# Two gate chunks moved to the mixer's entry, and way-up weights two tiles ahead with their low parts on GpSimd

## The chip, the cores and the metric

The kernel runs on one core of a Trainium2 chip. The metric is the device time of one execution in microseconds (us), the median of several runs. The core's engines work from separate instruction queues, each in order: TensorE (PE, its weight loads PEld), VectorE (DVE), ScalarE (ACT), GpSimd (POOL) and SyncE (SP), which here issues the DMAs.

## The reference

One step of a diffusion backbone with a single layer, on 1024 latent and 128 context tokens of width 1024 (1152 columns together, since the kernel keeps everything transposed). In short:

```python
x = x + 0.5 * m[2] * swiglu(modulate(x, norm_g[0], m[0], m[1]), *ffn1)
mix, ctx = token_mixer(modulate(x, norm_g[1], m[3], m[4]), ...)
x = x + m[5] * mix
x = x + 0.5 * m[8] * swiglu(modulate(x, norm_g[2], m[6], m[7]), *ffn2)
```

and in the token mixer

```python
qc, kvc, kr, hq, hf_f, hf_b, hi, hgate, ga, gr = split(h @ w_in)
...
merged = sigmoid(ga) * (o_attn @ w_up_attn) + sigmoid(gr) * (o_rec @ w_up_rec)
out = merged @ w_out
```

`o_attn` is softmax attention over compressed keys, `o_rec` a gated linear scan in both directions (HGRN2) with 8 heads, made from the projections hq (called q in the kernel), hf (f), hi (v) and hgate. ga and gr are the merge gates.

## The kernel before, in words

All matrices are float32. A product is made of three matmuls: each operand is split into a high part (a cast to fp32r on ACT) and a low part (the difference, on DVE or GpSimd), and high x high, high x low and low x high are added up in PSUM (`mm3`). A weight is so loaded by a DMA into a buffer `raw` (two of them), cast by ACT into `wh`, and subtracted into `wl` (three buffers each). `load_w` and `hl` do this; with `home="low"` or `"pieces"` the differences are on DVE in two halves.

The program is written as Python generators that yield after each piece; the order in which they are advanced is the order of the program. A planner then gives each engine its fixed order: of the instructions that its timing model holds ready, the one that stands first in the program. Buffers are reused by tags with a count; an instruction that writes into a buffer waits until the last one's readers are done.

**The mixer's entry** (`hgrn`). The 1152 columns are worked in three chunks of 384, in the order 2, 0, 1. The norm of the last chunk, 1, is still in work when the mixer begins: `self.tail` makes, one block of 128 rows at a time (8 steps), `xn` (L488, DVE), the high part `xh` (L489, ACT) and the low part `xl` (L490, DVE). Meanwhile TensorE makes the projections f, q and v of the first head pair. A projection chunk (`dense_g`, called by `proj_g`) is 24 matmuls of 384 columns in two halves of 12; it writes a PSUM bank of the tag `mm` (two banks) or, for some of the first chunks, `lv` (three). `rest` lists the order after f's and v's chunk 2: q and v and f and q by half chunks, up to v, f, q of chunk 1. The first eight half chunks of `rest` also advance `self.tail` by one step each, and from half chunk 11 on the scan's preparation `scan_pre` (its steps depend on f and q alone). Banks are read by ACT's sigmoid (L739) and, for q, also by DVE's product (L767); for v by a copy into a tile `t` (L778).

**The scan.** After `rest` the 8 heads are scanned in three chunks each. A scan step has small matmuls (L1068 with operands `KE`, `QP` from DVE, L1105), and between them `slots(k)` advances a chain of pending projections, `work`, by k half chunks: 7 or 8 in a step. `work_of(h)` lists what is in work for head h: the next head's f, at odd heads also the next pair's q and v, the output gate of a finished pair, and merge gates from `sgs` (16 generators `proj_sg`, each one weight and three chunks: sigmoid on ACT, stored to DRAM). What is left of the chain after the last scan step is run at the end, with the splitting of way-up weights for later (`split_up`), and then the last pair's output gate.

**The merge.** For each of 8 tiles m of 128 output rows, `up(m)` takes four quarters of 288 columns. The attention part is 12 matmuls of 288 columns, the recurrent part another 12 or, for two quarters, is read from DRAM as `mu`. DVE multiplies with the gates g and adds (L1688, L1690), ACT casts into `mh` (L1691), GpSimd makes `ml` (L1692). The weights of tiles 0 to 2 are loaded during attention; from then on `load_up_all` (L1425 to L1433) loads one: a DMA into `raw` (L1428), whose cast (L1677, ACT) and difference (L1678, DVE) make the first half of the weight, and two DMAs from DRAM (L1431), which bring the second half already split. After tiles 3 and 5, `down_group` adds two tiles' product with `w_out` to x: 192 matmuls, whose results DVE adds to x (L569) from three banks. `w_out`'s weights take the same `raw`, `wh` and `wl` buffers.

Of the kernel before, what the change touches and what calls it, by code (L numbers as in the profile page):

```python
# [21 lines left out]
KT = D // P  # L22
# [71 lines left out]
class Trunk:  # L94
# [761 lines left out]
    def hgrn(self):  # L856
        nc, pin = self.nc, self.tc.keep_in_program_order
        self.mmb = 2
        for tag, n in (("lv", 3), ("mm", 2), ("sm", 3)):
            self.pp.tile([P, 512], F32, tag=tag, bufs=n, name=tag)  # L860
        f32 = lambda n, sh: self.fp.tile(sh, F32, name=n)
        A, B = slice(0, 64), slice(64, P)
        self.kr = {m: f32(f"kr{m}", [P, CW]) for m in (8, 16, 32, 64)}
        self.XY = [f32(n, [P, 48, 8]) for n in "XY"]
        self.A1 = [f32(f"A1_{i}", [P, 3, G]) for i in range(2)]
        self.A2 = f32("A2", [P, 3, G])
        self.cnt, self.later, self.sigs = 0, [], []
        heads = [{} for _ in range(H)]
        pairs = [{} for _ in range(4)]
        sgs = [self.proj_sg(j) for j in range(2 * KT)]  # L870

        def feed(h):
            p = h // 2
            r = [self.proj_f(5 * p + h % 2, h, heads[h])]
            if h % 2 == 0:
                r += [self.proj_q(5 * p + 2, pairs[p]), self.proj_v(5 * p + 3, pairs[p])]
            return r

        def scan_of(h):
            p = h // 2  # L880
            if h % 2 == 0:
                pairs[p]["o"] = self.tt(F32, "oT")
            d = heads[h]
            d["pair"] = pairs[p]
            d["h"], d["QP"], d["As"] = h, self.tt(F32, "QP"), {}
            d["Gall"] = self.fp.tile([P, 9], F32, tag="Gall", bufs=2, name="Gall")
            return d

        def work_of(h):
            p = h // 2  # L890
            work = feed(h + 1) if h + 1 < H else []
            if h and h % 2 == 0:
                work = work + [sgs.pop(), self.beside(sgs.pop(), pairs[p - 1])]
                work += [self.proj_gate(5 * p - 1, p - 1, pairs[p - 1])]
            while len(work) < 4 - (h == 3) + (h == H - 1):
                work.append(sgs.pop())
            return chain(*work)

        pre = iter(())
        f, q, v = feed(0)  # L900

        def root_hook():
            next(v)
            next(self.tail)

        self.root_hook = root_hook
        for _ in range(2):
            next(f)
        next(v)

        def rest():
            for g in (q, v, f, q, v, f, q):
                for _ in range(2):
                    yield next(g)

        for i, _ in enumerate(rest()):
            if i < 8:
                next(self.tail)
            if i == 11:
                assert next(self.tail, 1)  # L920
                for t in self.XY:
                    pin(nc.vector.memset(t[:, :, 3:4], 1.0))
                d = scan_of(0)
                pre = self.scan_pre(d, ORDER[0])
            if i == 13:
                for t in self.A1 + [self.A2] + list(self.kr.values()):
                    pin(nc.vector.memset(t, 0.0))
            next(pre, None)
        for _ in pre:
            pass  # L930
        self.group()
        work = chain.from_iterable(map(work_of, range(H)))
        old = cur = out = last = None
        for p in range(H * NCH + 1):
            h, n = divmod(p, NCH)
            old, cur, pre = cur, None, iter(())
            if h < H:
                cur = self.scan_lev(d, ORDER[n])
            if p + 1 < H * NCH:
                h1, n1 = divmod(p + 1, NCH)  # L940
                while min(heads[h1].get("nf", 0), pairs[h1 // 2].get("nq", 0)) <= n1:
                    next(work)
                if n1 == 0:
                    last, d = d, scan_of(h1)
                pre = self.scan_pre(d, ORDER[n1])

            def slots(k):
                for _ in range(k):
                    next(work, None)
                    next(pre, None)  # L950

            self.group(old, cur)
            slots(3)
            self.group(old, cur, old, out)
            slots(2 + p % 2)
            self.group(cur, out, old)
            out = None
            if p and n == 0:
                out = self.scan_out(last if h < H else d)
                next(out)  # L960
            slots(2)
            for _ in pre:
                pass
        self.group(out, out)
        todo = list(range(KT // 2))
        for i, _ in enumerate(work):
            if i % 2 == 0 and todo:
                self.split_up(todo.pop(0))
        for p in todo:
            self.split_up(p)  # L970
        for n, _ in enumerate(self.proj_gate(19, 3, pairs[3])):
            if n == 0:
                self.group()
# [666 lines left out]
    def merge(self):  # L1640
        nc, a = self.nc, self.a
# [7 lines left out]
        def load_g(n=1):  # L1649
            for m, c in islice(parts, n):  # L1650
                g = self.half("g").rearrange("p (i n) -> p i n", i=2)
                pin(nc.sync.dma_start(g, self.sg[:, m, :, slice(*c)].rearrange("i p n -> p i n")))
                mu = None
                if REC[0] <= c[0] < REC[1]:
                    mu = self.fp.tile([P, QW], F32, tag="mu", bufs=4, name="mu")
                    pin(nc.sync.dma_start(mu, self.ahead[m][:, c[0] - REC[0] : c[1] - REC[0]]))
                gates.append((g, mu))

        def load_x(n):
            for k in range(len(self.x), min(len(self.x) + n, KT)):  # L1660
                t = self.tt(F32, f"x{k}")
                pin(nc.sync.dma_start(t[:, :T], self.xs[k]))
                self.x.append(t)

        def up(m):
            mh, ml = self.wide("mh", F32R), self.wide("ml", F32R)
            wh, wl = self.ups.pop(0)
            if m == 0:
                load_g(4)
            for n, c in enumerate(QORDER if m else first):  # L1670
                cs = slice(*c)
                g, mu = gates.pop(0)
                load_g()
                load_x(1)
                if 1 < m < KT - 1 and n == 0:
                    wh1, wl1, raw = self.load_up_all(m + 1)
                    nc.scalar.copy(wh1[:, :4], raw)  # L1677
                    nc.vector.tensor_sub(wl1[:, :4], raw, wh1[:, :4])  # L1678
                    self.ups.append((wh1, wl1))
                mt = []  # L1680
                for i in (1, 0):
                    if i and mu:
                        ps = mu
                    else:
                        ps = self.bank("up", "ups")
                        self.mm3(ps, [(wh[:, k], wl[:, k], *[t[:, cs] for t in hl[k]]) for k in range(4 * i, 4 * i + 4)])
                    t = self.fp.tile([P, QW], F32, tag="hf", bufs=3, name="mt") if i else ps
                    nc.vector.tensor_mul(t, ps, g[:, i])  # L1688
                    mt.append(t)
                nc.vector.tensor_add(mt[0], mt[1], mt[0])  # L1690
                nc.scalar.copy(mh[:, cs], mt[0])  # L1691
                nc.gpsimd.tensor_sub(ml[:, cs], mt[0], mh[:, cs])  # L1692
            return mh, ml
# [3 lines left out]
        for m in range(KT):  # L1697
            if m % 2 and m < KT - 1 and len(pend) > 1:
                homes = None, partial(self.tt, F32R)
                ws = [self.load_w(wo[f], 1, D, home=home, eng=nc.vector) for (f, _), home in zip(pend, homes)]  # L1700
            elif m == KT - 1:
                early = {i: self.load_w(wo[pend[i][0]], 1, D, home=homes[i], eng=nc.vector) for i in range(2)}
            pend.append((m, up(m)))
            if m % 2 and m < KT - 1 and len(pend) > 2:
                fs, hs = zip(*pend[:2])
                self.down_group(wo, fs, hs, 5, ws)
                pend = pend[2:]
# [742 lines left out]
```

## Time and profile before

| | us |
|---|---|
| median of three runs | 2833.44 |
| lowest and highest | 2833.11, 2836.21 |
| the profiled execution | 2831.82 |
| its span, first to last instruction | 2830.0 |

The profiled execution's mean granted TensorE clock is 0.995. TensorE is busy for 2763.6 us, DVE for 2037.8, ACT for 1302.9, GpSimd for 926.4. A row of the timeline has the start in us from the span's start, the duration in us, the engine, the line, the operation, the tile written and the tiles read, the shapes and the count; in brackets stand the engine's idle time before it and what ended it. A row of the waits reads: who waited for whom, us in total, times, the longest. A row of the groups reads: line, engine, operation, tiles, shape, count, then busy us, mean ns of one, then idle us before them with what ended most of it.

### The profile page before, as it was taken

Reading aid. Unit: us, or ns where it says so; the run is one execution under the profiler, and the core shown is the slowest. Engines: PE = TensorE matmul, PEld = TensorE weight load, DVE = VectorE, ACT = ScalarE, POOL = GpSimd, SP = SyncE. Lnnn points to the kernel's source line nnn. Section 1 sums busy time; section 2 is a strip of 40 time slices with the busy share of each in tenths; the row PEclk is TensorE's granted clock in tenths of the full one; section 3 lists DMA queues with packets and bytes.
Section 4 is the critical chain, followed back from the end, with each engine's and each line's share of the span. In section 5 each row is a group of like instructions: output and inputs, shape, how many; then the busy total and the mean of one; then the engine's idle time right before and its main releaser. Section 6 shows DMA issues by size and latency. Waiting matters only on the chain. (4 is left out here: it accounts for less than half of the span.)

```text
span 2830.0 us, 55726 instructions
## 1 busy us (share of the span) xinstructions
PE 2763.6 (98%) x21222; PEld 2633.5 (93%) x21222; DVE 2037.8 (72%) x4464; ACT 1302.9 (46%) x2696; POOL 926.4 (33%) x980
## 2 busy tenths in 40 slices
PE   8999999999999999999999999999999999999998
PEld 7999999999999998889998778689999999999997
DVE  7867777677678787877356777766766765568875
ACT  6533332321176676666436777741552322234332
POOL 0233232444222222222244444420414443423451
PEclk9999999999999999999999999999999999999999
DMA  6743443753121111112512001263454444358521
GB/s 261 228 130 118 130 125 118 260 180 117 57 82 57 45 63 38 66 41 84 192 60 98 19 15 30 84 232 104 154 171 130 145 156 134 116 164 253 164 85 67
DMA packets 219578, 337.64 MB, mean 119 GB/s; under 512 B 23664, under 2 KB 141360, under 8 KB 219312
## 3 DMA queue, kind: packets, MB, share of 16 engines
q1 hardware_dynamic: 219312, 334.10, 36.0%
q8 instruction: 167, 2.74, 0.4%
q14 instruction: 99, 0.81, 0.1%
HBM read 248.47 MB, written 85.54 MB: 118 GB/s over the span
## 5 line engine op out<-in xcount | busy, mean ns | idle before, releaser
L1902 PE MATMUL b<-xo,wo 128*128 128x288 f32 x3552 | 482.9, 295 | 0.0
L1902 PEld LDWEIGHTS b<-xo,wo 128*128 128x128 f32 x3552 | 474.8, 188 | 0.0
L1902 PE MATMUL b<-bh,wo 128*128 128x288 f32 x1776 | 366.0, 295 | 0.0
L539 PE MATMUL mm<-xh,wh 128*128 128x384 f32 x936 | 327.2, 350 | 5.5 <-DVE q L767 4.3
L541 PE MATMUL mm<-xh,wl 128*128 128x384 f32 x936 | 317.2, 339 | 0.0
L540 PE MATMUL mm<-xl,wh 128*128 128x384 f32 x936 | 316.6, 338 | 0.0
L1902 PEld LDWEIGHTS b<-bh,wo 128*128 128x128 f32 x1776 | 288.7, 188 | 0.0
L569 DVE SCALAR_TENSOR_TENSOR x<-dn,modt,x 128x256 f32<-128x256 f32 (+4 forms) x472 | 225.6, 499 | 83.8 <-PE dn L541 81.8
L1902 PE MATMUL b<-bl,wo 128*128 128x288 f32 x888 | 261.7, 295 | 0.0
L1876 ACT CAST wo<-raw 128x512 fp32r<-128x512 f32 x185 | 114.8, 621 | 221.1 <-issue 88.1
L539 PEld LDWEIGHTS mm<-xh,wh 128*128 128x128 f32 x936 | 176.4, 188 | 12.9 <-DVE q L767 5.5
L2103 PE MATMUL d<-xd,wd 128*128 128x288 f32 x1344 | 181.7, 297 | 5.0 <-DVE x L2090 3.0
L2103 PEld LDWEIGHTS d<-xd,wd 128*128 128x128 f32 x1344 | 180.0, 190 | 6.5 <-issue 4.4
L1877 DVE TENSOR_TENSOR wo<-raw,wo 128x512 fp32r<-128x512 f32 x185 | 127.4, 689 | 79.1 <-ACT wo L1876 76.5
L540 PEld LDWEIGHTS mm<-xl,wh 128*128 128x128 f32 x936 | 176.7, 189 | 0.9
L541 PEld LDWEIGHTS mm<-xh,wl 128*128 128x128 f32 x936 | 177.0, 189 | 0.0
L1599 POOL TENSOR_TENSOR ehl<-e,ehl 128x512 fp32r<-128x512 f32 x93 | 123.9, 1337 | 154.6 <-ACT ehl L1597 83.6
L393 DVE SCALAR_TENSOR_TENSOR junk<-wada,cb 128x512 bf16<-128x512 f32 x224 | 163.9, 732 | 5.5 <-DMA wada<-in_w_aT 4.6
L1902 PEld LDWEIGHTS b<-bl,wo 128*128 128x128 f32 x888 | 167.5, 189 | 0.0
L1872 POOL TENSOR_TENSOR ws<-raw 128x256 f32<-128x256 f32 x74 | 64.5, 892 | 283.1 <-DMA raw<-in_w 254.3
L539 PE MATMUL ps<-bh,wh 128*128 128x288 f32 (+1 forms) x448 | 135.7, 303 | 3.2 <-ACT bh L532 1.9
L1877 DVE TENSOR_TENSOR wo<-ws,wo 128x512 fp32r<-128x512 f32 x74 | 69.6, 940 | 92.4 <-ACT wo L1876 91.9
(477 smaller groups left out, 7163.9 us busy)
## 6 DMA issues: line engine op xcount, KB each, us to landing
raw<-in_w SPq DMA_DIRECT2D x148, 256.0 KB, 3.5
wada<-in_w_aT SPq DMA_DIRECT2D x112, 256.0 KB, 3.1
raw<-in_w SPq DMA_DIRECT2D x42, 512.0 KB, 3.8
raw<-in_w_in SPq DMA_DIRECT2D x41, 512.0 KB, 3.5
xr<-xd SPq DMA_DIRECT2D x56, 288.0 KB, 3.8
hr<-hs SPq DMA_DIRECT2D x26, 576.0 KB, 5.7
hb<-hd SPq DMA_DIRECT2D x44, 288.0 KB, 3.8
hs<-et SPq DMA_DIRECT2D x84, 144.0 KB, 2.3
```

What stands on the lines that cost most here:

```text
L393: nc.vector.scalar_tensor_tensor(junk, ws[n % 2], 1.0, cs[s], ALU.mult, ALU.mult, accum_out=o)
L539: pin(nc.tensor.matmul(ps, wh, xh, start=start and i == 0, stop=False))
L540: pin(nc.tensor.matmul(ps, wh, xl, start=False, stop=False))
L541: self.last_mm = nc.tensor.matmul(ps, wl, xh, start=False, stop=stop and i == n - 1)
L569: nc.vector.scalar_tensor_tensor(self.x[m][:, a:b], ps[:, a - lo : b - lo], self.modt[:, gm, m, s : s + 1], self.x[m][:, a:b], ALU.mult, A ...
L1599: eng.tensor_sub(el, e, eh)
L1872: nc.gpsimd.tensor_tensor(o[:, c], x[:, c], y[:, c], op)
L1876: nc.scalar.copy(wh, src[i])
L1877: nc.vector.tensor_sub(wl, src[i], wh)
L1902: nc.tensor.matmul(ps, w[:, k], x[:, k, :QW], start=first, stop=last, skip_group_check=home != i)
L2103: nc.tensor.matmul(ps, w[:, k], xv, start=start, stop=stop, skip_group_check=home != i)
```

## The change

In the mixer's entry one merge gate (`fill`) is taken from the list of 16, and four half chunks of it, that is its chunks 2 and 0, are put into `rest` ahead of v's, f's and q's chunk 1. Its third chunk stays, as the first gate in head 0's work. In the merge the weights of tiles 3 and 4 are loaded in tiles 1 and 2 instead of 2 and 3; those of tiles 5 to 7 stay where they were. All five differences go from DVE to GpSimd.

```diff
@@ work_of
                 work += [self.proj_gate(5 * p - 1, p - 1, pairs[p - 1])]
+            if not h:
+                work.append(fill)
             while len(work) < 4 - (h == 3) + (h == H - 1):
                 work.append(sgs.pop())
@@ hgrn
         next(v)
 
+        fill = sgs.pop()
+
         def rest():
-            for g in (q, v, f, q, v, f, q):
+            for g in (q, v, f, q, fill, fill, v, f, q):
                 for _ in range(2):
                     yield next(g)
@@ merge, up
-                if 1 < m < KT - 1 and n == 0:
-                    wh1, wl1, raw = self.load_up_all(m + 1)
+                if m in (1, 2, 4, 5, 6) and n == 0:
+                    wh1, wl1, raw = self.load_up_all(m + (2 if m < 3 else 1))
                     nc.scalar.copy(wh1[:, :4], raw)
-                    nc.vector.tensor_sub(wl1[:, :4], raw, wh1[:, :4])
+                    nc.gpsimd.tensor_sub(wl1[:, :4], raw, wh1[:, :4])
                     self.ups.append((wh1, wl1))
```

## The prediction

> **What bounds the kernel now.** I read the page first, then the busy time by stages, then the waits of TensorE inside the stages that the change touches, and last the engines' order in time around each wait.
>
> ```profile
> span 2830.0 us, 55726 instructions
> PE 2763.6 (98%) x21222; PEld 2633.5 (93%) x21222; DVE 2037.8 (72%) x4464; ACT 1302.9 (46%) x2696; POOL 926.4 (33%) x980
> ```
>
> TensorE is busy for 98% of the span, and the change neither adds nor removes a matmul. So only three things can pay: TensorE's idle time, stretches in which its granted clock is low, and new waits. The profiled execution took 2831.8 us, 1.8 us more than its span; the median of the runs is 2833.4. I make the sum against the profiled one and take the difference off the median. A measurement of this kernel can tell about 0.2% from no change, 5.7 us.
>
> The stages at the mixer's entry, from the view of busy time by window (window, its length, busy time and instructions of PE, PEld, DVE, ACT, POOL, granted clock, DMA):
>
> ```profile
> 832.26:840.68 8.42, 8.42 (x50) 8.42 (x49) 7.13 (x18) 4.31 (x10) 1.33 (x3) 1.00 0.01 2
> 840.68:849.46 8.78, 6.77 (x26) 4.74 (x25) 6.16 (x16) 4.52 (x8) 0.00 (x0) 0.83 0.00 0
> 849.46:859.64 10.18, 10.18 (x50) 10.14 (x49) 7.94 (x17) 7.07 (x14) 2.33 (x4) 0.81 0.00 1
> 859.64:879.64 20.00, 18.02 (x190) 16.58 (x189) 19.24 (x49) 13.94 (x32) 5.24 (x7) 1.00 0.08 28
> 880.64:884.06 3.42, 3.42 (x11) 3.42 (x12) 2.69 (x9) 3.33 (x8) 1.63 (x4) 0.50 0.34 122
> ```
>
> The first window holds f's and q's chunk 0: 48 matmuls in 8.42 us, 0.175 each. The second is v's chunk 1, the first work on the last chunk of the normed input: 24 matmuls that should take 4.2 us take 8.78, 4.6 lost. In the third, f's and q's chunk 1 take 10.18 instead of 8.42, 1.8 lost to a clock of 0.81. In the fourth TensorE idles 2.0 us while DVE is busy for 19.24 of 20, and the fifth runs at half clock: 1.7 lost. Who ended these waits, in the view of waits (the first two lines at the last chunk, the third in the scan's first steps):
>
> ```profile
> PE lv L539 <- ACT xh L489: 1.6, 3, 0.7
> PE lv L540 <- DVE xl L490: 0.4, 2, 0.2
> PE lv L1068 <- DVE QP L1105: 1.9, 2, 1.7
> ```
>
> TensorE runs out of normed input first, then of the scan's operands from DVE. The merge, in windows from the end of its third tile on, and its waits:
>
> ```profile
> 1890.50:1892.78 2.28, 0.16 (x2) 0.00 (x1) 1.23 (x4) 0.95 (x2) 0.93 (x2) 1.00 1.10 377
> 1892.78:1902.16 9.38, 9.38 (x71) 9.38 (x71) 6.73 (x12) 2.33 (x3) 1.10 (x2) 1.00 0.43 142
> 1902.16:1906.35 4.19, 3.30 (x24) 2.86 (x22) 3.50 (x9) 1.82 (x4) 2.57 (x3) 1.00 0.89 262
> 1906.35:1929.60 23.25, 23.25 (x175) 23.25 (x175) 15.83 (x36) 1.96 (x3) 0.00 (x0) 1.00 0.38 134
> 1948.90:1955.84 6.94, 5.04 (x39) 4.81 (x37) 3.99 (x10) 1.49 (x3) 2.42 (x3) 1.00 0.92 289
> 1955.84:1959.25 3.41, 3.41 (x15) 3.41 (x16) 1.62 (x5) 0.00 (x0) 0.00 (x0) 0.50 0.79 254
> ...
> PE ups L539 <- ACT wh L1677: 2.1, 1, 2.1
> PE dn L539 <- DVE x L569: 1.9, 1, 1.9
> PE ups L541 <- DMA wl<-wrec: 0.9, 1, 0.9
> PE ups L539 <- DVE mt L1690: 0.4, 1, 0.4
> ```
>
> A tile's way-up takes about 9.4 us, a matmul of the down group 23.25 / 175 = 0.133. Idle are 2.1 us ahead of tile 3, 0.9 in the window of tile 4's first matmuls, 0.4 later, 1.9 in the second down group, which a half-clock stretch follows (1.7 more).
>
> **Part 1: two gate chunks ahead of the last chunk.** Moved are 48 matmuls (8.4 us), their weight load of one DMA, one ACT cast and two DVE differences, two sigmoids on ACT and two stores on SP. The same work leaves the scan's filler later, so the matmuls cost nothing by themselves; the question is how much idle time they fill. They are long enough for all of it: v's chunk 1 would start at 840.7 + 8.4 = 849.1, when its input is complete. But the moved chunks write the two banks named mm, which f's and q's chunk 0 hold until ACT and DVE have read them:
>
> ```profile
> 841.96 0.47 ACT L739 ACTIVATE sg<-mm 128x384 f32<-128x384 f32 x1
> 848.51 0.55 DVE L767 TENSOR_TENSOR q<-mm,sg 128x384 f32<-128x384 f32 x1
> ```
>
> ACT and DVE run in a fixed order, and there these reads stand behind steps of the last chunk's norm, which the change leaves where it is. If that order stays, the first moved chunk starts at 841.96 + 0.47 = 842.4 instead of 840.7 (1.7 us of waiting) and ends at 846.6; the second waits for 848.51 + 0.55 = 849.1 (2.4 us). So 4.1 us of idle time stay.
>
> Whether the clock drops as well depends on how the wait falls. In the merge 1.9 us of idle time in the 6.9 us ahead were enough for a stretch of 3.41 us at 0.50. I count half of one such stretch, 0.85. Of 4.6 + 1.8 = 6.4 lost, 5.0 remain: a gain of 1.4, between 0.6 (a whole slow stretch) and 6.4 (the reads come earlier). [...]
>
> A cost on the other side: the third weight buffer now holds the moved gate, so the next f's weights, loaded ahead today, wait for v's last matmul. There are then 48 matmuls (8.4 us) of f and q to hide a cast, two differences and the queues; I put it at 0, with 1 us as the lower bound below. On SP the two stores wait for the sigmoids; behind them queue only loads of weights that are used after q's chunk 1.
>
> **The scan's first steps.** DVE is late there:
>
> ```profile
> 866.88 0.36 DVE L1075 COPY_PREDICATED A<-mask,lv 128x96 f32<-128x96 uint8 x2
> ```
>
> This reads products that TensorE makes right behind q's chunk 1, from 859.64 on, so DVE comes some 6 to 7 us late; it does the preparation of scan chunk 0 and the memsets first. With TensorE 8.4 us later at that point, DVE has done these by then. I count 2.5 of the 2.0 + 1.7 = 3.7 us as gained, between -1 and 3.7.
>
> **The rest of the scan.** Each scan step takes a fixed number of half chunks from the row of pending projections, so its amount of work stays; but all that follows comes four half chunks earlier, and meets another state of DVE. The waits between 900 and 1385:
>
> ```profile
> PE mm L539 <- DVE q L767: 4.3, 3, 2.3
> PE lv L1068 <- DVE QP L1105: 3.0, 4, 1.4
> PE ops L1164 <- ACT kT L1122: 1.6, 2, 0.8
> PE vt L785 <- ACT t L778: 1.3, 2, 0.7
> ```
>
> These 10.2 us are redrawn; I take 0 with 4 us either way. At the scan's end the leftover is four half chunks shorter:
>
> ```profile
> 1385.44:1398.16 12.72, 12.72 (x72) 12.56 (x72) 0.00 (x0) 1.47 (x3) 1.00 0.88 314
> ...
> 1392.56 1.29 DVE L346 TENSOR_TENSOR wl<-raw,wh 128x512 fp32r<-128x512 f32 x2 [7.62 <-ACT wh L342]
> ```
>
> Of the 72 matmuls 12 are the last gate's first half; it starts at 1385.44 + 60 x 0.175 = 1395.9, and its weights are ready at 1393.85. Needed 8.4 us earlier, they would be 6.3 us late if their load stayed. But that load hangs on weight buffers which earlier gates release, and these also come 8.4 us of TensorE's work earlier. I take 0, at worst -6.3.
>
> **Part 2: weights of tiles 3 and 4 two tiles ahead.** Tile 3's load today:
>
> ```profile
> 1882.44 0.33 SPq L1428 DMA_DIRECT2D raw<-in_w_up  x1
> ```
>
> It moves up by one tile of 9.4 us on SP, to about 1873: three DMAs among the g and x loads. Its buffer is free since tile 0. Its cast and difference then lie under tile 2, and the 2.1 us go. Tile 4's load, today ahead of tile 3's end, goes up by one tile too, and the 0.9 us go. Queued behind these DMAs on SP are loads of g for four quarters ahead; three issues of 0.3 to 0.4 us do not reach them. What is late next is the first down group's weights: they take the buffers that tile 2 and the loads ahead of them release. I leave 0.5 us for that.
>
> **Low parts on GpSimd.** The five differences, and what waits today:
>
> ```profile
> L1678 DVE TENSOR_TENSOR wl<-raw,wh x5: 691/692/866, 1892.8 to 1954.6; 128x512 fp32r<-128x512 f32 x5
>   ACT wh L1677: 7.0, 5
> ...
>   DMA raw<-in_w_up: 9.6, 3
> ...
> 1954.57 0.69 DVE L1678 TENSOR_TENSOR wl<-raw,wh 128x512 fp32r<-128x512 f32 x1 [2.56 <-ACT wh L1677]
> 1955.18 1.49 DVE L569 SCALAR_TENSOR_TENSOR x<-dn,modt,x 128x288 f32<-128x288 f32 x4
> ...
> L1599 POOL TENSOR_TENSOR ehl<-e,ehl x93: 1270/1291/2828, 1539.1 to 1856.8; 128x512 fp32r<-128x512 f32 x93
> L1692 POOL TENSOR_TENSOR ml<-mt,mh x32: 791/807/967, 1867.7 to 2000.8; 128x288 fp32r<-128x288 f32 x32
> ```
>
> DVE stood 7.0 us idle ahead of these five, each time for ACT's cast, and ACT stood 9.6 us ahead of three of the casts for their DMA. At 1954.57 four results of the down group queue behind one; with three banks full TensorE stops for 1.9 us and its clock halves for 1.7. On GpSimd the same difference takes 1.3 us (the same shape at L1599) against 0.69; behind it only ml differences of 0.8 us queue, which the next down group needs, one or two tiles later. So 1.9 + 1.7 + 0.4 go. Together the merge gains 2.1 + 0.9 + 0.4 + 1.9 + 1.7 - 0.5 = 6.5, between 4 and 7.
>
> [...]
>
> ```profile
> L1688 DVE TENSOR_TENSOR mt<-mu,g 128x288 f32<-128x288 f32 x16 | 8.8, 567 | 0.7 <-POOL ml L1692 0.7
> L1688 DVE TENSOR_TENSOR mt<-ups,g 128x288 f32<-128x288 f32 x16 | 7.3, 456 | 7.7 <-PE ups L541 7.7
> ```
>
> The product with both inputs in SBUF takes 567 ns beside GpSimd's ml, the one with a PSUM input 456. Five differences of 1.3 us could hold DVE for 6.5 us at most; DVE is busy for 6.73 of 9.38 us in tile 3's window, so 1.3 us in a tile fits.
>
> **Sum.** 1.4 + 2.5 + 0 + 6.5 = 10.4 us: 2831.8 becomes 2821.4, the median 2833.4 becomes 2823.
>
> **Rivals.** (a) The reads of the two banks come early, since they alone hold TensorE: entry and first steps pay in full, 6.4 + 3.7 + 6.5 = 16.6, 2817. For it: ACT is idle for 4.3 of 8.78 us there. Against it: the norm's steps keep their place. (b) The scan gives back what the entry brings, by late weights at its end (6.3) or redrawn waits (4): 6.5 + 3.9 - 6.3 = 4.1 or 6.4, so 2827 to 2829. If the moved chunks were not ahead of v in the order that results, entry and scan give 0, and the time is 2827 as well. (c) GpSimd's low parts hold DVE's two-input products or its own ml back, and the merge keeps its waits: 3.9 alone, 2829.5. For it the 567 ns above, against it DVE's free time. [...] (d) Slower: q's products. Nine chunks of q run in the scan; 3 of them wait 1.4 us in the mean today. If the shift brought the other six into DVE's full stretches as well, each with a slow stretch of 1.7 behind it, that costs 6 x 3.1 = 18.6 against 10.4 gained: 2841.6. It decides from the fourth such chunk on (3.1 x 4 = 12.4).
>
> **Chances.** The forecast 0.48, (a) 0.15, (b) 0.23, (c) 0.08, (d) 0.06. The range reaches from (a), with a clock to spare, to past (b) and (c): 2815 to 2832, leaving out (d) and some of the scan's spread. Faster by over 0.2% means below 2827.7: the forecast, (a) and a third of (b), 0.69. Slower is (d), 0.06; within 0.2% 0.25.
>
> **What would show it.** Right: at about 842 and 849 the first matmuls of the moved chunks wait for ACT L739 and DVE L767, v's chunk 1 runs without a wait; no wait on ACT wh ahead of tile 3; no DVE wl in the merge, and no slow stretch in the second down group. Wrong: moved chunks without waits (a); waits at the last gate or on q between 900 and 1400 that exceed those above (b, d); merge waits on POOL (c).

## The result and the profile after

| | us |
|---|---|
| median of six runs after | 2823.01 (2821.65 to 2824.73) |
| median of six runs of before beside them | 2833.28 (2832.25 to 2836.21) |
| ratio | 0.9963, 95% interval 0.995 to 0.9976 |
| the profiled execution after, its span | 2824.73, 2822.9 |

The kernel became 10.3 us faster: 0.37%, between 0.24% and 0.5%. Timed two more times, the same kernel was 8.5 and 8.9 us faster than before beside it (0.32% both times). After the new line in `work_of` lines stand two lower than before, behind `fill = sgs.pop()` and its empty line four lower: L1068 is L1072, L1105 is L1109, L1678 is L1682, L1688 is L1692, L1832 is L1836.

The page's first lines show the same 21222 matmuls, 5 us less busy time of TensorE, and five instructions that went from DVE to POOL:

```profile
span 2822.9 us, 55736 instructions
PE 2758.5 (98%) x21222; PEld 2635.4 (93%) x21222; DVE 2034.1 (72%) x4459; ACT 1304.0 (46%) x2696; POOL 933.4 (33%) x985
```

Busy time by window (columns as in the prediction): first moved chunk and the wait behind it, second moved chunk, v, f and q's chunk 1, the scan's first steps up to the first transposes of k, then the merge's way-up of tiles 0 to 3 and the stretch up to its last way-up matmul.

```profile
843.87:851.32 7.45, 4.48 (x25) 4.16 (x25) 7.25 (x16) 5.26 (x12) 2.84 (x4) 1.00 0.00 1
851.32:855.64 4.32, 4.32 (x25) 4.32 (x25) 4.26 (x10) 2.39 (x6) 0.00 (x0) 1.00 0.13 46
855.64:868.26 12.62, 12.62 (x74) 12.58 (x73) 8.94 (x28) 7.07 (x15) 1.60 (x2) 1.00 0.18 58
868.26:894.10 25.84, 25.84 (x335) 24.36 (x333) 21.36 (x54) 18.57 (x40) 4.63 (x9) 1.00 0.14 42
1861.27:1898.30 37.03, 37.03 (x278) 37.03 (x279) 21.11 (x48) 9.30 (x20) 15.84 (x18) 1.00 1.01 365
1898.30:1984.60 86.30, 86.30 (x648) 86.19 (x648) 62.41 (x132) 14.94 (x26) 21.66 (x20) 1.00 0.38 119
```

The third row, v, f and q's chunk 1, is 12.62 us without idle time at full clock, where before 8.78 + 10.18 = 18.96 stood. In the fourth TensorE is busy for 25.84 of 25.84 us: the first steps' wait and slow stretch are gone. In the two rows of the merge it is busy throughout. What is left of waits at the entry, in the view of TensorE's waits from 838 to 895:

```profile
PE mm L539 <- DVE q L767: 3.0, 1, 3.0
PE mm L539 <- ACT sg L739: 1.4, 1, 1.4
```

They are the two waits of the forecast, in its places and on its releasers. The same view for the rest of the scan, 895 to 1385:

```profile
PE lv L1072 <- DVE QP L1109: 4.3, 3, 3.4
PE mm L539 <- DVE sg L841: 3.9, 2, 2.0
PE vt L785 <- ACT t L778: 3.6, 2, 2.4
PE lv L1072 <- POOL QP L1109: 0.3, 1, 0.3
```

They add up to 12.1 us, before to 12.9, but in 8 waits instead of 15, and the longest three have a stretch at half clock behind them, where before's profile has one such stretch in the scan:

```profile
1057.88:1061.30 3.42, 3.42 (x12) 3.42 (x12) 2.37 (x4) 2.21 (x5) 2.80 (x4) 0.50 0.55 168
1173.94:1177.35 3.41, 3.41 (x11) 3.41 (x12) 3.32 (x7) 3.11 (x8) 0.95 (x2) 0.50 0.37 131
1225.14:1228.55 3.41, 3.41 (x13) 3.41 (x13) 2.73 (x9) 1.81 (x7) 0.00 (x0) 0.50 0.02 5
```

To compare all runs I took four marks from each trace: the first transposes of k in the scan, the merge's first way-up matmul, FFN2's first matmul, TensorE's last. Differences to before by stage, in us; "entry" is taken from a matmul ahead of the mixer to the transposes of k, and the 8.4 us of moved matmuls (4.2 where one chunk is moved) are taken off there and put back in "scan, attention".

| kernel | ahead of the mixer | entry and first steps | scan, attention | merge | FFN2 and end | median's difference |
|---|---|---|---|---|---|---|
| after | +1.6 | -5.3 | -1.2 | -7.6 | +5.0 | -10.3 |
| after, second profile | +1.9 | -2.5 | -2.8 | -7.7 | +1.0 | -8.5 |
| after, third profile | +1.8 | -5.3 | -0.2 | -7.7 | +1.2 | -8.9 |
| entry part alone | +2.9 | -3.8 | -2.9 | -1.9 | +1.0 | -4.6 |
| merge part alone | +1.5 | -0.9 | +0.6 | -8.1 | +0.3 | -8.9 |
| loads ahead alone | +2.4 | -1.3 | +0.5 | -6.9 | -0.6 | -6.7 |
| GpSimd alone | +2.5 | -0.9 | -0.6 | -5.6 | +1.9 | -4.4 |
| moved chunks on lv | +2.4 | -5.0 | -2.4 | -7.7 | +0.4 | -12.0 |
| moved chunks on lv, again | +2.9 | -6.1 | -2.8 | -7.7 | +0.3 | -11.1 |
| lv and less DVE work | +1.4 | -2.4 | -3.4 | -7.7 | -0.2 | -8.2 |
| chunks behind q | +1.1 | -0.6 | +1.6 | -7.7 | +0.8 | -5.2 |
| one chunk ahead | +1.4 | -1.2 | -10.3 | -7.9 | +0.8 | -16.0 |
| one ahead, one behind q | +1.1 | -4.5 | -0.3 | -7.7 | +2.6 | -9.7 |

The last column is the median of five or more runs against that of before's runs beside them. The changed merge takes 7.6 to 8.1 us less in every kernel that has both its halves, and in after's three profiles the same to 0.1 us. In every trace the mixer begins 1.1 to 2.9 us later than in the one profile of before, in kernels too that change nothing ahead of it, so that column says something of this one profile and not of the change. The same holds for part of two more columns. The three kernels that leave the entry as it was are 0.9 to 1.3 us shorter there, and none of them has before's stretch at half clock in the first steps; the kernel that leaves the merge as it was is 1.9 us shorter there, also without before's stretch. Against these profiles after gains about 1 us less at the entry and 1.9 less in the merge than the table has.

### The profile page after: what moved, and what is told of

It reads as the page before. It is cut to its first block, busy times and chain, and to the rows that moved or that the text cites. A ratio compares the mean times of both kernels' runs of the same rounds, so it can differ in the third digit from the quotient of the medians.

```text
span 2822.9 us, 55736 instructions
## 1 busy us (share of the span) xinstructions
PE 2758.5 (98%) x21222; PEld 2635.4 (93%) x21222; DVE 2034.1 (72%) x4459; ACT 1304.0 (46%) x2696; POOL 933.4 (33%) x985
```

## The experiments

### Each part alone

The entry part alone leaves the merge as it was; the merge part alone leaves the entry.

```diff
 entry part alone: the edits in work_of and rest, and none in up
 merge part alone: the edit in up, and none in work_of and rest
```

> The entry part alone, the merge as before. My theory: two waits of 1.4 and 3.0 us ahead of the moved chunks replace the 6.4 us lost at the last chunk, the scan's first steps lose their 2.0 us wait and the slow stretch (3.9 in the changed kernel's trace), the rest of the scan changes by about 1: 4 to 6 us faster than before. Rival (the scan gives back what the entry brings): within 1 us of before.

> The merge part alone, the entry as before. My theory: the waits of 2.1, 0.9, 0.4 and 1.9 us and the slow stretch of 1.7 go: 7 to 8 us faster than before. Rival (GpSimd's low parts hold DVE or the next tile back): under 3 us.

Measured: 2827.35 us (ratio 0.9983, 0.9975 to 0.9992) and 2823.1 (0.997, 0.9959 to 0.9981), against 2831.99. The entry part's 4.6 us lie in the range that I expected, the merge part's 8.9 (8.1 by the marks) just above it. The marks agree by stage with the kernel after: the merge part's 8.1 us come in the merge; the entry part took 1.9 off there, because no slow stretch followed the waits this time. That GpSimd's differences hold the merge back, rival (c), falls: no wait of TensorE but the 0.6 at the first tile is left. The medians' gains do not add up: 4.6 + 8.9 = 13.5 against 8.5 to 10.3 of after. By the stages they nearly do: 6.7 us in entry and scan of the one and 8.1 in the merge of the other make 14.8, against 13.0 to 14.1 in after's profiles, of which 2.9 to 6.6 us are lost again in the outer columns. Whether part of that belongs to the change, the runs do not settle; each median is known to some 3 us either way. So the times do not tell the whole change (0.9963, 0.9968, 0.9968) from its merge part alone (0.997). That the entry part pays rests on its run alone and on the stages.

### The merge part's two halves

```diff
 loads ahead alone
-                if 1 < m < KT - 1 and n == 0:
-                    wh1, wl1, raw = self.load_up_all(m + 1)
+                if m in (1, 2, 4, 5, 6) and n == 0:
+                    wh1, wl1, raw = self.load_up_all(m + (2 if m < 3 else 1))
 GpSimd alone
-                    nc.vector.tensor_sub(wl1[:, :4], raw, wh1[:, :4])
+                    nc.gpsimd.tensor_sub(wl1[:, :4], raw, wh1[:, :4])
```

> The kernel before with one half of the merge part: the weights of tiles 3 and 4 loaded two tiles ahead, their low parts still on DVE. My theory: the merge's gain of 8.1 us (merge part alone) is two separate losses. The loads ahead remove only the waits ahead of tiles 3 and 4 (2.1 and 0.9 us), so the time falls by about 3 us, to a ratio near 0.999; the wait of 1.9 us in the second down group and the slow stretch behind it stay, because a low part of a later tile still stands on DVE between that group's results. Rival: the loads ahead alone remove that wait as well (the low part comes early enough that nothing queues behind it), and the gain is 7 to 8 us, ratio near 0.997.

> The kernel before with the other half of the merge part: the low parts on GpSimd, the loads where they were. My theory: the wait of 1.9 us in the second down group, the slow stretch of 1.7 us behind it and the 0.4 us go, a gain of about 4 us, ratio near 0.9986; the wait ahead of tile 3 (2.1 us, for ACT's cast) stays and the one ahead of tile 4's last third grows by the longer difference on GpSimd (1.3 against 0.69 us), to about 1.5 us. Rival: the loads are what counts, DVE drains its results in time once they come, and without them nothing is gained; or GpSimd's longer difference makes the waits ahead of tiles 3 and 4 so long that a new slow stretch eats the gain: a ratio within 0.001 of 1.

Measured: 2824.86 us (0.9975, 0.9966 to 0.9985) and 2827.16 (0.9982, 0.9973 to 0.9991), against 2831.55. The waits of TensorE in the merge, with the loads ahead alone:

```profile
PE dn L539 <- DVE x L569: 1.0, 1, 1.0
PE ups L539 <- DVE mt L1688: 0.6, 1, 0.6
```

and with GpSimd alone:

```profile
PE ups L539 <- ACT wh L1677: 1.3, 1, 1.3
PE ups L539 <- DMA wh<-wrec: 0.7, 1, 0.7
PE ups L539 <- DVE mt L1688: 0.6, 1, 0.6
```

My sharing out of the gain fell. The loads ahead alone take 6.9 of the 8.1 us, as the rival had it: of the wait in the second down group 1.0 of 1.9 stays, and no slow stretch follows it in this profile. GpSimd alone takes 5.6: the wait of 2.1 us ahead of tile 3 stays (0.7 + 1.3), as expected, but the 0.9 us ahead of tile 4's last third went where I expected them to grow; why is open. 6.9 + 5.6 = 12.5 is more than 8.1, because both remove the slow stretch of 1.7 us, the wait at tile 4 and part of the wait in the down group. Whichever half is made first seems to bring most of the gain, and the other, made second, 1.2 or 2.5 us. The overlap is not the slow stretch alone: against the merge of the entry part's profile, which is before's without that stretch, the halves bring 5.0 and 3.7 us and both together 6.2.

### Where the entry's loss goes

First the moved chunks write the three banks named lv, which are free there:

```diff
-            s = self.sigm((yield from self.proj_g(w, c)))
+            s = self.sigm((yield from self.proj_g(w, c, "lv" if j == 15 and c != ORDER[-1] else "mm")))
```

> The changed kernel with its two moved chunks on the lv banks, of which one is free and the others are read early, instead of the mm banks. My theory, that only the banks' readers hold these chunks: the two waits (1.4 and 3.0 us) go, v's chunk 1 starts 8.4 us after q's chunk 0, when its input is nearly complete: 3.5 to 4.5 us faster than the changed kernel. Rival: the last chunk's norm is what all wait for, so the wait moves to v's chunk 1 or to the first f of the scan: under 1.5 us faster than the changed kernel.

Measured: 2820.02 us (0.996, 0.9948 to 0.9972). Both waits at the entry are gone and q's chunk 1 is done some 5 us earlier, but the transposes of k are not: -5.0 in the table against -5.3. In the first steps stand new waits:

```profile
PE lv L1072 <- DVE QP L1109: 1.9, 1, 1.9
PE mm L539 <- DVE q L767: 1.3, 1, 1.3
```

and a slow stretch follows. The theory that free banks are worth 3.5 to 4.5 us fell: against before beside it this kernel gained 12.0 us, after 8.5 to 10.3. The timeline of DVE shows what the bank waits for: q's product stands behind the reciprocals of the next scan chunk, which wait for ACT, while q's chunk was done at 863.95.

```profile
867.79 0.71 DVE L1019 TENSOR_TENSOR X<-fs,X 128x48 f32<-128x48 f32 x2 [2.34 <-ACT X L1017]
868.54 1.05 DVE L1020 RECIPROCAL Y<-X 128x144 f32<-128x144 f32 x1
869.51 1.29 DVE L1022 RECIPROCAL X<-Y 128x192 f32<-128x192 f32 x1
...
870.95 0.56 DVE L767 TENSOR_TENSOR q<-mm,sg 128x384 f32<-128x384 f32 x1
```

Entry and first steps look like one budget: before's profile lost 6.4 + 3.7 = 10.1 us there, and after and this kernel both win about half of it, with waits at other places. What sets that budget is not shown; the run with less work on DVE, below, was to show it. Timed again beside the kernel after:

> The kernel after with the moved chunks on the banks named lv, the same as in the run with that change alone, now timed beside the kernel after in one call. My theory: it is no faster than after, its median within 1.5 us, since the scan's first transposes of k come at the same time and the 3 us between the two medians of separate calls are the spread of FFN2 between executions. Rival: the free banks are worth 2 to 3 us.

It took 2819.46 us (2818.48 to 2821.5; 0.9961, 0.9947 to 0.9974) against after's 2821.68 (2820.33 to 2824.61; 0.9968, 0.9956 to 0.9979). That is 2.2 us less with runs that overlap; against after's third profile the marks show 0.8 us less at the transposes of k and 2.7 in the scan. My 1.5 us were too few, and whether it is a real gain stays open.

Then DVE gets less to do: the low parts of three early weights, 3 x 1.3 us, go to GpSimd.

```diff
 with the moved chunks on lv
-        w = self.load_w(self.a["w_in"][i], KT, P, home="own" if h == 0 else "low")
+        w = self.load_w(self.a["w_in"][i], KT, P, home="own" if h == 0 else None if h == 1 else "low")
-        w = self.load_w(self.a["w_in"][20 + j], KT, P, home="low")
+        w = self.load_w(self.a["w_in"][20 + j], KT, P, home=None if j > 13 else "low")
```

> The kernel after with the moved chunks on the banks named lv (as in the run with that change alone) and, besides, the low parts of three early weights (the last two gates and the second f) on GpSimd instead of DVE: 3 x 1.3 = 3.9 us of DVE's work less around the entry and the scan's first steps. My theory, formed after the lv run: DVE's work sets the pace up to the scan's first transposes of k, so that what the entry gains by free banks is lost again in the first steps; with DVE relieved the waits there (1.3 us on q's product, 1.9 us on the scan's operand, a slow stretch of 1.7) shrink, and the first transposes of k come 2 to 4 us earlier than in the lv run, measured from the start of the moved work. Rival: it is the fixed place of q's product and of the operands in DVE's order, behind two reciprocals, not the amount of its work: the waits stay within 0.7 us of what they were. A second rival: GpSimd, at 2.6 us for a whole weight, delivers the low parts late, and the last third of f's or a gate's chunks waits for it: slower by 1 to 3 us.

Measured: 2823.35 us (0.9966, 0.9954 to 0.9979); the transposes of k come 2.6 us later than with lv alone, not earlier. The waits up to there:

```profile
PE mm L539 <- ACT sg L739: 3.9, 1, 3.9
PE lv L1072 <- DVE QP L1109: 1.0, 1, 1.0
```

A stretch of 6.83 us at half clock follows the longer one, where lv alone had one of 3.41 in the first steps; that alone is 1.7 of the 2.6 us. None of the three had this. The sigmoid of f's chunk 1 stands in ACT's order behind copies of `kr`, and these wait for DVE's `KE`, which is late for two reasons. The planner, with other work to place, put the scan's preparation behind steps of the norm: its first product of `Kb` starts at 851.61 here and at 844.83 with lv alone. And two products of `KE` took 2.1 us longer beside GpSimd's new difference. The row of GpSimd in this kernel:

```profile
863.73 2.35 POOL L354 TENSOR_TENSOR wl<-raw,wh 128x1024 fp32r<-128x1024 f32 x1
```

two rows of DVE in this kernel:

```profile
851.61 0.55 DVE L1027 TENSOR_TENSOR Kb<-kk,X 64x384 f32<-64x384 f32 x1
...
863.87 2.81 DVE L1109 TENSOR_TENSOR KE<-KE,T 64x192 f32<-64x192 f32 x2
```

and the same two with lv alone:

```profile
844.83 0.54 DVE L1027 TENSOR_TENSOR Kb<-kk,X 64x384 f32<-64x384 f32 x1
...
860.89 0.73 DVE L1109 TENSOR_TENSOR KE<-KE,T 64x192 f32<-64x192 f32 x2
```

Two products that take 0.73 us with lv alone take 2.81 here, and end 0.6 us after GpSimd's instruction does (863.73 + 2.35 = 866.08). So this run does not tell whether the amount of DVE's work sets the pace: of the 3.9 us taken off DVE 2.1 came back at once in these two products, and the order changed with it. That stays open.

The chunks can also stand behind q's chunk 1, where they help the first steps alone:

```diff
-            for g in (q, v, f, q, fill, fill, v, f, q):
+            for g in (q, v, f, q, v, f, q, fill, fill):
```

> The changed kernel with the two moved chunks behind q's chunk 1 instead of ahead of v's. Theory for the scan's first steps, that they gain because DVE has 8.4 us more before them: the 6.4 us at the last chunk are lost as before, the first steps still run without their 2.0 us wait and without a slow stretch, so 1 to 2 us slower than the changed kernel. Rival, that the first steps gain from the shorter stall ahead of them: they lose about 3.9 as before, 5 us slower than the changed kernel.

Measured: 2826.81 us (0.9983, 0.9975 to 0.9992). The entry loses what it lost before, the moved chunks wait 2.6 us for q's product with a slow stretch behind them, and the first steps run without a wait; the gain up to the transposes of k is 0.6 us, 2 to 5 us less than after's. So DVE's head start does clear the first steps, as the theory had it, but the theory left out the moved chunks' own wait, and by its size the loss is nearer to the rival's. The scan behind, in the same order as after's, was 1.6 us slower than before here, with three stretches at half clock besides the entry's two.

### The same kernel profiled again

> The kernel after itself, timed beside the other runs of this call and profiled a second time. The ratio to before should be 0.996 to 0.997 again. In the profile the merge and the entry should show the same waits as in the first profile of after, to 0.3 us: they follow from the order of the instructions. For the rest of the scan and the second FFN my theory is that the waits and slow stretches differ from execution to execution though the order is the same (FFN2 loses 0 to 5 us in one execution against another); the rival is that the losses of 5.4 us in FFN2 belong to the program after and come back at the same places.

> The kernel after itself beside the other two, as their measure: ratio to before 0.996 to 0.997; a third profile, to see how much of the half-clock stretches at the entry and of the waits in FFN2 is the same from one execution to the next.

The medians were 2823.08 and 2821.68 us, both at a ratio of 0.9968 (0.9956 to 0.9981, and to 0.9979). The waits at the entry came back as 1.4 and 3.0, and the merge to 0.1 us. What differs is the clock: after the same waits TensorE ran 6.8 us at half clock in the second profile, and in the first and third not at all.

```profile
850.91:857.73 6.82, 6.17 (x19) 6.17 (x20) 6.74 (x16) 2.71 (x6) 0.35 (x1) 0.50 0.08 29
```

That costs about 3.4 us, and the table's difference between -5.3 and -2.5 is 2.8. Where I had counted 0.85 it was 0, 3.4 and 0, and 1.7 in the entry part's profile, which has the same order and the same two waits there.

The traces show how the wait lies. In before's profile the stretches at half clock begin 10, 73, 325, 537 and 579 whole steps of 3.413 us behind the first one, in after's first 34, 49, 223, 454, 473 and 515. Counted on in these steps, one begins at 849.67 in after's first profile and one at 850.91 in the second, so the steps lie otherwise against the program there. These are the steps that hold the wait of 3.0 us, two in the first profile and one in the second:

```profile
846.26:849.67 3.41, 2.09 (x12) 1.76 (x11) 3.26 (x9) 2.46 (x6) 1.50 (x3) 1.00 0.01 2
849.67:853.08 3.41, 1.76 (x10) 1.77 (x11) 3.41 (x6) 2.45 (x6) 1.34 (x2) 1.00 0.00 0
```

```profile
847.50:850.91 3.41, 1.09 (x7) 0.76 (x5) 3.29 (x8) 2.19 (x7) 2.49 (x4) 1.00 0.01 2
```

In the first profile the wait falls into two steps, TensorE is busy for 2.09 and 1.76 us of 3.41, and the clock stays; in the third likewise (2.04 and 1.81). In the second nearly the whole wait falls into one step with 1.09 us busy, and the half clock begins at its end. That the busy time within a step decides is my reading of these rows; what sets the clock is not shown.

FFN2's loss of 5.0 in the first profile did not come back (1.0 and 1.2). Its waits in the first profile, then in the second:

```profile
PE d L2107 <- DVE x L2094: 4.2, 3, 2.3
PE d L2107 <- DVE su L2112: 2.0, 1, 2.0
PE ps L539 <- DVE sl L1836: 1.4, 1, 1.4
```

```profile
PE d L2107 <- DVE x L2094: 3.5, 6, 1.5
PE d L2107 <- DVE su L2112: 2.0, 1, 2.0
PE ps L539 <- DVE sl L1836: 0.7, 1, 0.7
```

The same pairs wait, 1.4 us less in total and in shorter pieces. And FFN2 has two stretches at half clock in the first profile (at 2607.53 and 2672.39), none in the second and one each in the third and in before's, 1.7 us apiece.

### One chunk instead of two

```diff
-            for g in (q, v, f, q, fill, fill, v, f, q):
+            for g in (q, v, f, q, fill, v, f, q):
```

> The kernel after with one chunk of the gate ahead of v's last chunk instead of two; the other one runs later, in the scan. The first moved chunk must wait about 1.4 us for ACT's sigmoid as in after (it stands in the same place) and end at about 848; v's last chunk then waits for the last part of its normed input, 0.5 to 1.5 us, instead of the second moved chunk's 3.0 us. My theory (DVE's work sets the pace up to the scan's first transposes of k, entry and first steps are one budget): the entry looks better by 1 to 2 us, the first steps then wait on DVE again, 2 us and perhaps a slow stretch of 1.7; measured from a common point before the entry the first transposes of k come 2 to 4 us later than they would with two, net of the moved work, and the ratio to before is 0.997 to 0.998. Rival: the second chunk brings nothing, since its wait of 3.0 us costs as much as it fills; then the gain is that of after, ratio 0.9965, with no new wait in the first steps.

Measured: 2814.59 us (2812.9 to 2817.15), ratio 0.9944 (0.9931 to 0.9956), where after beside it has 2821.68. It is the fastest of all kernels here, and nothing I expected gives that. Up to the transposes of k the theory's mechanism came out, the first steps waiting on DVE again, with a stretch of 3.41 us at half clock; the waits there:

```profile
PE lv L1072 <- DVE QP L1109: 1.9, 1, 1.9
PE mm L539 <- DVE q L767: 1.5, 1, 1.5
PE mm L539 <- ACT sg L739: 1.4, 1, 1.4
PE lv L539 <- ACT xh L489: 1.0, 1, 1.0
PE lv L540 <- DVE xl L490: 0.3, 1, 0.3
```

That is a gain of 1.2 us up to there, 4 less than after's 5.3 (1.3 less than in after's second profile). The merge is after's. What is new, 10.3 us, comes from the scan behind, whose waits from 895 to 1385 are now

```profile
PE mm L539 <- DVE sg L841: 3.8, 5, 1.6
PE lv L1072 <- DVE QP L1109: 1.5, 2, 1.0
PE vt L785 <- ACT t L778: 1.0, 2, 0.8
PE lv L1072 <- DVE A L1114: 0.2, 1, 0.2
```

6.5 us instead of 12.1, none over 1.7, and the clock does not drop in that stretch at all. Against after's first profile that is 5.6 us of waits and three slow stretches of 1.7, 10.7 together, where the table has 9.1. The table's row is one execution, but the clock is not that execution's luck alone: the mean granted clock was 0.997 to 0.999 in the five executions of this kernel and 0.995 to 0.997 in the 17 of after.

Is it the entry or the scan? The last run has the entry of this kernel and the scan of after, since the second chunk stands ahead of the scan as well:

```diff
-            for g in (q, v, f, q, fill, fill, v, f, q):
+            for g in (q, v, f, q, fill, v, f, q, fill):
```

> The kernel after with one chunk of the gate ahead of v's last chunk, as in the run with one chunk, and the second one right behind q's last chunk, ahead of the scan; from the scan's first step on the order of the work is that of after. It tells apart where the 7 us come from by which one chunk alone beat the kernel after. My theory: from the rest of the scan. With one chunk ahead all pending projections come two half chunks earlier than before, with two they come four earlier, and where each of them meets DVE's load decides (12 us of waits and three stretches at half clock in after, 6.5 us and none with one chunk). Then this kernel, whose scan is after's, loses the gain: from the first transposes of k to the merge as in after (960 to 962.6 us), a ratio of 0.996 to 0.998; at the entry the waits of the run with one chunk (1.4, 1.0, 0.4), in the first steps none, since the second chunk gives DVE 4 us to catch up. Rival: the 7 us come from the entry (the wait of 3.0 us there is gone) and what follows from it, and this kernel has them too: a ratio of 0.9945.

Measured: 2820.38 us (0.9965, 0.9952 to 0.9979). The gain is gone. VectorE, ScalarE and GpSimd run the scan in after's order, and its waits are after's, each to 0.1 us:

```profile
PE lv L1072 <- DVE QP L1109: 4.3, 3, 3.4
PE mm L539 <- DVE sg L841: 3.9, 2, 2.0
PE vt L785 <- ACT t L778: 3.6, 2, 2.4
PE lv L1072 <- POOL QP L1109: 0.3, 1, 0.3
```

So it is the place of the pending projections in the scan, with the order that the planner makes of it, and not the entry: one chunk earlier than before the scan gains 10 (one profile), two chunks earlier between -1.6 and 3.4 (nine profiles). Why this place is better than the others is read from the waits alone; no run varies it further. In the first steps, where I expected no wait, two of 0.9 were left.

## Why the prediction was right, and where only its number was

**The two waits at the entry.** Right in place and releaser. 842.4 and 849.1 were forecast, which is 844.0 and 850.7 with the 1.6 us by which all of this execution lies later; the chunks started at 843.87 and 851.32. v's chunk 1 ran without a wait, and q's chunk 1 ended 8.6 us later than before, of which 8.4 are moved work and 1.6 came from ahead: a gain of 1.4, as forecast. That the size fits so well is luck: the two waits took 0.3 us more than the 4.1 forecast, 0.6 more went outside the listed waits, and no slow stretch followed in place of the 0.85. In the second profile, with 6.8 us at half clock, the same sum gives a loss of 1.3, outside the 0.6 to 6.4 that I had put down; I had priced the wait with one slow stretch at most. Rival (a) fell: the reads of the two banks kept their place. The run on lv shows that (a) would not have paid in full either, for the first steps take it back.

**The weights of the next f.** Right: no wait of TensorE on them in any profile of after.

**The first steps.** The mechanism was right, the size too small: 2.5 counted of 3.7, 3.9 came, no wait and no slow stretch in any of the three profiles. Of before's 3.7 the 1.7 were that execution's: in the three other profiles with the old entry the first steps have no slow stretch, and against them after gains 2.3 to 3.6 us. Where the chunks help only here, the first steps run clean as well.

**The rest of the scan.** Taken as 0 with 4 us either way; it was -1.2, -2.8 and -0.2, attention included. As a forecast of this change that is right. As a judgement of what that stage can do it was wrong: one chunk less moves it by 8 to 10 us, more than the entry and the first steps together. "Redrawn" was the right word; 4 us as its bound had no row behind it, and the 10.2 us of waits were the four longest lines of a view that adds up to 12.9. Rival (b) fell for the two-chunk shift, and the last gate did not wait for its weights at the scan's end. Rival (d) fell: of q's 4.3 us of waits before none is left in after, the waits changed to other tiles.

**The merge.** The term of 6.5 measured 7.6. The reserve of 0.5 for the down group's weights was not needed, and the restart at tile 3 cost a little more than its listed wait: the step from one matmul to the next was 2.3 us longer than the usual 0.13, for a wait of 2.1. Right in total, the attribution fell: not 3.0 for the loads and 4.0 for GpSimd, but 6.9 and 5.6, which overlap. A product can take longer beside GpSimd, 1.47 us in the row below for 0.46, but that falls into DVE's free time. A row of DVE and the row of GpSimd beside it, after:

```profile
1935.74 1.47 DVE L1692 TENSOR_TENSOR mt<-mu,g 128x288 f32<-128x288 f32 x1
```

```profile
1935.60 1.30 POOL L1682 TENSOR_TENSOR wl<-raw,wh 128x512 fp32r<-128x512 f32 x1 [2.58 <-ACT wh L1681]
```

A product of 0.46 us that starts 0.14 us behind one of the five differences takes 1.47. No wait of TensorE comes of it.

**The sum.** 2823 was forecast and measured. That it fits to the microsecond is luck. By stages it is 14.1, 13.0 and 13.2 us in the three profiles, not 10.4, and 2.9 to 6.6 us are missing in stages that I had put at nothing, ahead of the mixer and in FFN2. Timed two more times, the gain was 8.5 and 8.9 us. The order of the instructions is the same in these stages before and after. With a single profile of before it stays open how much of it is that execution's luck and how much follows from the change. One sum of mine was off: the forecast, (a) and a third of (b) make a chance of 0.71, not 0.69.

## What to carry to other kernels

A filler that is put ahead of one wait also shifts all work that is pending behind it; try the shift in several sizes, for here the size that fills the visible hole least well (one chunk) was 7 us ahead of two on the same banks and 5 ahead of two on free ones, and its gain came in the scan behind. Halves of a change whose gains overlap cannot be priced from the waits that each removes: a wait that becomes shorter can lose its slow stretch too (in the second down group 1.9 us had one behind it, 1.0 with the loads ahead alone had none), so that the first half seems to do nearly all. A stretch at half clock that one profile shows is not a price either: the same wait of 3.0 us at the entry had 6.8 us of it behind it in one execution and none in two. And work that is given from VectorE to GpSimd can come back on VectorE: of 3.9 us given away 2.1 came back in two of its products.

## What the runs showed of the hardware

The clock. A wait of the same length in the same place is followed by no stretch at half clock in two executions and by 6.8 us of it in a third (after's entry, 1.4 and 3.0 us of waits within 7.5 us). The stretches measured in the middle of the kernel are 3.41 us or twice that (in before's profile 6.83 from 846.51 and 3.41 from 880.64, 1095.68, 1955.84 and 2679.47). Within that trace, and within after's first, they begin whole steps of 3.413 us apart, and where a step begins differs between executions (849.67 and 850.91 at after's entry), so a stretch in one profile is counted in that profile's own steps. How little use of a step goes with half clock is not shown as one share: in before's profile a step with TensorE busy for 0.48 of it (from 1890.99) was followed by full clock, others at 0.50 (from 877.23) and 0.55 (from 843.10) by half, with the ends of matmuls as the profile models them. The six runs of after lie 3.1 us apart (2821.65 to 2824.73); how much of that is such stretches is not shown.

VectorE beside GpSimd. The 567 ns against 456 at before's L1688 is an average, whose 16 rows have a median of 454 ns and a longest of 1005. In two other places products of DVE with two inputs in SBUF started 0.14 us behind a difference on GpSimd and ended 0.6 and 0.3 us behind its end: two products of together 0.73 us took 2.81 beside one of 2.35 (lv and less DVE work), and one of 0.46 took 1.47 beside one of 1.30 (after). In both cases the loss, 2.1 and 1.0 us, is below the length of GpSimd's instruction. Why they take longer is not shown.
